# A decoder layer whose front runs in two passes of four token blocks instead of three of two, four and two

## The chip, the core and the metric

One core of a Trainium2 chip runs the whole layer as one launch. The metric is the device time of one execution in microseconds, the median of three runs. The core has five engines that run beside each other, each with its own list of instructions in a fixed order: PE (matmul), DVE (vector), ACT (scalar functions), POOL (here it only issues gathers) and SP (here it only issues transfers).

## The reference

Sequence 1024, width 1024, all float32. In short:

```python
h = x
h = h + hybrid_mixer(rms_norm(h, norm_mix), w_in, conv_w, ..., w_out)   # conv group + gated DeltaNet
h = h + memory_cross_attention(rms_norm(h, norm_x), rms_norm(mem, norm_mem), w_xq, w_xkv, w_xo)
h = h + peer_ffn(rms_norm(h, norm_ffn), w_query, sub_keys, expert_u, expert_v)
return rms_norm(h, norm_final)

def peer_ffn(xn, ...):            # 8 heads x 16 best of 128 x 128 experts: 128 rows for each token
    q = xn @ w_query; scores = q against two sets of 128 keys; two top-16, then top-16 of their sums
    u = expert_u[idx]; act = gelu(xn . u); y = sum(gate * act * expert_v[idx])
```

The DeltaNet part is a recurrence over the sequence: the state after one block of tokens goes into the next. `expert_u` and `expert_v` hold 16384 rows of 4 KB each.

## The kernel before

The 1024 tokens are eight blocks of 128. Four of them (2 to 5) get their experts densely: all 16384 experts are multiplied (`dense`), and a table of gates, written to DRAM by `densify`, zeroes those not chosen. The other four (0, 1, 6, 7) get their experts by gathering: for each token 128 rows of `expert_u` and 128 of `expert_v`, 512 KB for each slot of a block.

The front (everything up to the queries of the retrieval) runs per `Chunk` of blocks: `inproj` (28 weights of 128 columns from `w_in`), `invert` and `recur` (the recurrence, a pair of blocks at a time), `outproj`, `cross`, `queries`. Every weight of 512 KB is loaded by SP into `wraw`, split into `whi` by ACT (L242) and `wlo` by DVE (L244), and multiplied three times (L248 to L250). The chunks are blocks 0 and 1, then 2 to 5, then 6 and 7, so the front's weights pass three times, with 256, 512 and 256 columns.

`queries` ends with `best_keys`, where `top16` (L817 to L821) finds the best keys on DVE. `route_close` turns them into gates and row numbers. `gather_u` multiplies gathered rows with the token on DVE (L935). The sum over `expert_v` has two forms: `gather_v` adds row by row on DVE (L1020), `gather_p` lets PE multiply 32 columns of weights with the gathered rows, four products at once (L971), for two gathers. The bit mask `VD` says which blocks take DVE: 194 are blocks 1, 6 and 7. Gathered rows land in the pool `gp`, in `NG` = 6 buffers of 4 KB a partition. `densify` makes one-hot tiles on DVE (L1050 to L1053, in a tile of the pool `qp`, named `unit`) and multiplies them on PE (L1059).

The order on each engine: the parts are Python generators; `merge` takes steps of several of them in proportion to the numbers beside them, and `G1` to `G5` say how many of the 1036 gather steps go beside which part. `tc.high_priority` (in `at`) shifts the priority by which the framework's scheduler then places instructions. The engines obey the order that comes out of it; nothing overtakes.

Of the kernel before, what the change touches and what calls it, by code (L numbers as in the profile page):

```python
# [41 lines left out]
NSLIP, CLOSE, PACE = 4, 3, 517  # L42
G1, G2, G3, G4, G5 = 98, 90, 107, 17, 60
A5 = -1
C4, T5 = 61, 92
NSHORT, NRAW, NHI, NLO, NG, LU, LV, VD = 6, 3, 2, 2, 6, 1, 1, 194
PG1, PG2, PG3, PT, PR, PD = 100, -25, 0, 0, 0, 0
# [29 lines left out]
def merge(*gens):  # L77

    done = [0] * len(gens)
    live = [True] * len(gens)  # L80
    while any(live):
        j = min((i for i in range(len(gens)) if live[i]), key=lambda i: done[i] / gens[i][1])
        try:
            yield next(gens[j][0])
            done[j] += 1
        except StopIteration:
            live[j] = False


def run(*gens):  # L90
    for g in gens:
        for _ in g:
            pass
# [19 lines left out]
def _body(ctx, tc, I, out, dbg, front_only):  # L113
# [20 lines left out]
    def unit():  # L134
        return qp.tile([P, 4, T], F32, name="unit")
# [640 lines left out]

    def queries(c):

        t0, NB, T = c.t0, c.nb, c.T
        hv = c.h  # L780
        rstd = normalise(hv)
# [12 lines left out]
        for b in range(NB):  # L794
            routes[c.b0 + b] = Route(c.b0 + b)
        for hh in range(4):
            pair = []
            keys = sp.tile([P, 2, P], F32, name="keys")
            nc.sync.dma_start(keys, I["keysT"][:, 2 * hh:2 * hh + 2])
            for i in (2 * hh, 2 * hh + 1):  # L800
                ps = yield from proj_ct(I["w_pq"][i], x, T)
                pair.append(short()[:, :T])
                act(pair[-1], ps, AF.Copy)
                yield
            for b in range(0, NB, 2):
                yield from best_keys(c.b0 + b, hh, pair, keys, b * P)

# [217 lines left out]
    def densify(r, n):  # L1025
# [18 lines left out]
        for q in range(4):  # L1044
            st = [unit().rearrange("p a t -> p (a t)").rearrange("p (j t) -> p j t", t=32) for _ in range(2)]
            for v in range(0, 32, 8):
                ts = slice(32 * q + v, 32 * q + v + 8)
                hot = unit().bitcast(F16)
                oi, oj, *part = (hot[:, i].rearrange("p (g i t) -> p g i t", g=4, t=2) for i in range(4))
                tt(oi, iota8, pairs(num[:, 0, ts]), op=OP.is_equal)  # L1050
# [107 lines left out]

    ca, cb, cc = Chunk(0, 2), Chunk(2, 4), Chunk(6, 2)

# [5 lines left out]

    def tables(first):
        for n in range(4):
            yield from route_close(routes[first + n])
        for n in range(4):  # L1170
            yield from densify(routes[first + n], n)

# [10 lines left out]
    next(mem)  # L1183
    run(merge((invert(ca, (0, 1)), 17), (steps(mem, 13), 13)))
    run(merge((chain(recur(ca, 0), recur(ca, 1)), 10), (mem, 27)))
    run(chain(outproj(ca), cross(ca)))
    ib = inproj(cb)
    qa = queries(ca)
    if A5 >= 0:
        next(qa)  # L1190
        next(ib)
        run(merge((qa, 24), (steps(ib, A5), A5)))
    else:
        run(qa)
    if front_only:
# [3 lines left out]
    ga = at(pg, gathers(0))  # L1199
    tables2 = at("PT", tables(2))  # L1200
    for part, n, g in ((ib, 83 - max(A5, 0), G1), (recurrence(cb), 52, G2),
                       (chain(outproj(cb), cross(cb)), 59, G3)):
        run(merge((steps(ga, g), g), (part, n)))
    pg['now'] = 'PG2'
    banks["both"] = False
    qb = queries(cb)
    next(qb)
    rest = at("PR", chain(inproj(cc), recurrence(cc), outproj(cc), cross(cc), queries(cc)))
    run(merge((steps(ga, G4), G4), (qb, 32), (steps(rest, C4), C4)))
    run(merge((steps(ga, G5), G5), (tables2, T5), (rest, 195 - C4)))  # L1210

# [54 lines left out]
```

## Time and profile before

| | |
|---|---|
| median of three runs | 3339.02 us (3330.76 to 3339.60) |
| the profiled execution | 3335.89 us, span 3334.1 us |
| busy share of the span | PE 84%, DVE 81%, ACT 40%, POOL 40% |
| gathers (L918 and L964) | 1024, 536.94 MB of 890.34 MB in all |

The trace times start at the first instruction, and a stage is named by the weights that DVE begins to split at its start. The stages run from 0 to 370.6 (blocks 0 and 1), to 645.0 (input projection of blocks 2 to 5), to 886.4 (their recurrence), to 1064.0 (their output projection and attention), to 1348.0 (their queries mixed with the input projection of blocks 6 and 7), to 1577.0 and 1796.4 (the rest of blocks 6 and 7, beside the tables), to 3212.0 (dense part) and to the end.

### The profile page before, as it was taken

The page shows a single profiled execution, that of the slowest core. Times are in us where ns is not written, and L with a number is a line of the kernel's source. Part 1 is how long each engine was busy: PE and PEld are TensorE (multiplying, and loading weights), DVE is VectorE, ACT ScalarE, POOL GpSimd, SP SyncE. Part 2 cuts the span into 40 slices and gives each one's busy share as a digit, 9 for nine tenths or more (in the row PEclk, how much of TensorE's full clock was granted, in tenths as well). Part 3 has the DMA queues.
Part 4 walks back from the last instruction along what each step waited for, and adds up shares of the span by engine and source line. Part 5 has one row for each costly group of instructions (what it writes and reads, how often), then busy time and mean ns, then how long its engine had stood idle before and what let it go on. Part 6 is the DMA issues. An engine that isn't in the chain of part 4 may idle for free.

```text
span 3334.1 us, 42650 instructions
## 1 busy us (share of the span) xinstructions
PE 2784.7 (84%) x14826; PEld 2307.0 (69%) x14826; DVE 2693.7 (81%) x5527; ACT 1339.8 (40%) x2367; POOL 1324.6 (40%) x1028
## 2 busy tenths in 40 slices
PE   7898588877888877466777999999999999999950
PEld 7887466666555656465656888888888888888840
DVE  6654899978655788997668999888888888887888
ACT  5444333322232323334443554444444444444430
POOL 0000046746545441000000456556655555665665
PEclk9999788989998888788788999999999999999975
DMA  4344368959988884113455889999999999999998
GB/s 166 113 147 140 120 233 302 354 184 324 328 309 306 308 291 155 64 77 143 154 190 188 297 307 363 347 344 346 345 336 342 348 348 349 343 339 339 348 329 315
DMA packets 325495, 890.34 MB, mean 267 GB/s; under 512 B 27424, under 2 KB 96672, under 8 KB 321184
## 3 DMA queue, kind: packets, MB, share of 16 engines
q0 software_dynamic: 147456, 536.94, 44.3%
q1 hardware_dynamic: 177824, 350.69, 30.0%
q8 instruction: 116, 1.90, 0.2%
q14 instruction: 99, 0.81, 0.1%
HBM read 838.77 MB, written 48.76 MB: 266 GB/s over the span
## 4 chain that ended last, share of the span: by engine, by line
PE 43%; DVE 3%; issue 2%; DMA 1%; ACT 1%; POOL 1%; SPq 0%; POOLq 0%; DVEq 0%; ACTq 0%
PE ps L248 7%; PE ps L249 7%; PE ps L250 7%; PE po L248 7%; PE po L250 7%; PE po L249 7%; DMA g<-expert_v,g_ii 1%; POOL g L918 1%; DVE unit L1053 0%; DMA d_s<-kmd 0%; PE ps L1059 0%; DVE g_y L1020 0%; DVE wlo L244 0%; ACT whi L242 0%; DVE unit L1050 0%
## 5 line engine op out<-in xcount | busy, mean ns | idle before, releaser
L918 POOL DMA_INDIRECT g<-expert_u,g_ii x512 | 666.4, 1302 | 898.9 <-DVE t_s L820 434.4
L918 POOL DMA_INDIRECT g<-expert_v,g_ii x384 | 518.5, 1350 | 930.8 <-ACT g L1001 536.0
L242 ACT ACTIVATE whi<-wraw 128x1024 fp32r<-128x1024 f32 x452 | 479.9, 1062 | 836.0 <-PE ps L249 413.5
L244 DVE TENSOR_TENSOR wlo<-wraw,whi 128x1024 fp32r<-128x1024 f32 x452 | 552.4, 1222 | 321.7 <-ACT whi L242 319.4
L935 DVE SCALAR_TENSOR_TENSOR g<-g,xn 128x1024 f32<-128x1024 f32 x512 | 617.4, 1219 | 121.0 <-DMA g<-expert_u,g_ii 111.7
L250 PE MATMUL ps<-unit,wlo 128*128 128x512 f32 (+1 forms) x1784 | 653.3, 367 | 39.4 <-DVE wlo L244 39.3
L248 PE MATMUL ps<-unit,whi 128*128 128x512 f32 (+1 forms) x1784 | 659.1, 370 | 13.7 <-ACT whi L242 5.5
L249 PE MATMUL ps<-unit,whi 128*128 128x512 f32 (+1 forms) x1784 | 651.6, 365 | 0.0
L1020 DVE SCALAR_TENSOR_TENSOR g_y<-g,g_a,g_y 128x1024 f32<-128x1024 f32 x381 | 488.1, 1281 | 20.1 <-DMA g<-expert_v,g_ii 12.7
L249 PE MATMUL po<-wlo,unit 128*128 128x512 f32 x1136 | 444.0, 391 | 0.0
L250 PE MATMUL po<-whi,unit 128*128 128x512 f32 x1136 | 443.9, 391 | 0.0
L250 PEld LDWEIGHTS ps<-unit,wlo 128*128 128x128 f32 x1784 | 350.3, 197 | 98.6 <-DVE wlo L244 45.0
L248 PEld LDWEIGHTS ps<-unit,whi 128*128 128x128 f32 x1784 | 351.6, 197 | 76.7 <-ACT whi L242 11.0
L249 PEld LDWEIGHTS ps<-unit,whi 128*128 128x128 f32 x1784 | 351.5, 197 | 50.0 <-issue 0.8
L248 PE MATMUL po<-whi,unit 128*128 128x512 f32 x1136 | 383.1, 391 | 0.0
L249 PEld LDWEIGHTS po<-wlo,unit 128*128 128x128 f32 x1136 | 214.1, 188 | 48.3 <-issue 2.7
L250 PEld LDWEIGHTS po<-whi,unit 128*128 128x128 f32 x1136 | 214.0, 188 | 46.8 <-issue 2.5
L248 PEld LDWEIGHTS po<-whi,unit 128*128 128x128 f32 x1136 | 214.0, 188 | 45.8 <-issue 1.1
L1113 ACT ACTIVATE unit<-po 128x512 f32<-128x512 f32 x256 | 152.6, 597 | 150.1 <-PE po L250 144.8
L964 POOL DMA_INDIRECT g<-expert_v,g_y x128 | 139.4, 1089 | 161.3 <-DVE g L935 57.5
L1100 ACT ACTIVATE po<-unit 128x512 f32<-128x512 f32 x248 | 144.5, 605 | 0.0
L1059 PE MATMUL ps<-unit 128*128 128x128 f16 x1024 | 86.8, 239 | 52.3 <-DVE unit L1053 38.7
(391 smaller groups left out, 4053.1 us busy)
## 6 DMA issues: line engine op xcount, KB each, us to landing
wraw<-u_t SPq DMA_DIRECT2D x128, 512.0 KB, 7.1
wraw<-expert_v SPq DMA_DIRECT2D x128, 512.0 KB, 7.0
wraw<-w_in SPq DMA_DIRECT2D x84, 512.0 KB, 4.6
gd<-unit SPq DMA_DIRECT2D x32, 1024.0 KB, 5.9
unit<-gd SPq DMA_DIRECT2D x32, 1024.0 KB, 15.1
wraw<-w_out SPq DMA_DIRECT2D x24, 512.0 KB, 4.2
wraw<-w_xq SPq DMA_DIRECT2D x24, 512.0 KB, 4.4
wraw<-w_xo SPq DMA_DIRECT2D x24, 512.0 KB, 4.9
```

What stands on the lines that cost most here:

```text
L242: act(hi, raw, AF.Copy)
L244: tt(lo, raw, hi.bitcast(F32), op=OP.subtract)
L248: nc.tensor.matmul(ps, lh, rh, start=first, stop=False, skip_group_check=open_)
L249: nc.tensor.matmul(ps, lh, rl, start=False, stop=False, skip_group_check=open_)
L250: nc.tensor.matmul(ps, ll, rh, start=False, stop=last, skip_group_check=open_)
L918: nc.gpsimd.indirect_dma_start(out=g, out_offset=None, in_=I[table], in_offset=bass.IndirectOffsetOnAxis(ap=ii[:, k:k + 1], axis=0))
L935: stt(g, g, 1.0, xn, op0=OP.mult, op1=OP.mult, accum_out=r.a[:, k:k + 1])
L964: nc.gpsimd.indirect_dma_start(out=g, out_offset=None, in_=I["expert_v"], in_offset=bass.IndirectOffsetOnAxis(ap=iT[:, t:t + 1], axis=0))
L1020: stt(y, g, a[:, k:k + 1], y, op0=OP.mult, op1=OP.add)
L1059: nc.tensor.matmul(ps[:, u * P:(u + 1) * P], part[i][:, g, :, t], oj[:, g, :, t], start=i == 0, stop=i == 1)
L1100: act(pss[b], y[b][:, half * 512:(half + 1) * 512], AF.Copy)
L1113: act(y[b][:, half * 512:(half + 1) * 512], pss[b], AF.Copy)
```

## The change

The chunks become blocks 0 to 3 and 4 to 7. `queries` gets a first block and a count, since the second chunk does its retrieval in two halves: blocks 4 and 5, which go to the dense part, then 6 and 7. The tables of blocks 2 and 3 are made beside the recurrence of the second chunk, those of blocks 4 and 5 beside its last queries. The gathers of blocks 0 and 1 begin after the first chunk's queries, and 460 of their steps stand ahead of the dense part instead of 372. `VD` is 192, so block 1 is summed on PE like block 0. In `densify` the one-hot tile moves from the pool `qp` to two of the six buffers of the gathers.

```diff
-G1, G2, G3, G4, G5 = 98, 90, 107, 17, 60
-A5 = -1
-C4, T5 = 61, 92
-NSHORT, NRAW, NHI, NLO, NG, LU, LV, VD = 6, 3, 2, 2, 6, 1, 1, 194
+G1, G2, G3, G4, G5 = 100, 110, 140, 40, 70
+NSHORT, NRAW, NHI, NLO, NG, LU, LV, VD = 6, 3, 2, 2, 6, 1, 1, 192
...
-    def queries(c):
+    def queries(c, b0, NB):
...
-                hot = unit().bitcast(F16)
-                oi, oj, *part = (hot[:, i].rearrange("p (g i t) -> p g i t", g=4, t=2) for i in range(4))
+                hot = [gp.tile([P, D], F32, name="g").bitcast(F16) for _ in range(2)]
+                oi, oj, *part = (h[:, D * i:D * i + D].rearrange("p (g i t) -> p g i t", g=4, t=2)
+                                 for h in hot for i in range(2))
...
-    ca, cb, cc = Chunk(0, 2), Chunk(2, 4), Chunk(6, 2)
+    ca, cb = Chunk(0, 4), Chunk(4, 4)
...
-    def tables(first):
-        for n in range(4):
+    def tables(first, n0):
+        for n in range(2):
             yield from route_close(routes[first + n])
-        for n in range(4):
-            yield from densify(routes[first + n], n)
+        for n in range(2):
+            yield from densify(routes[first + n], n0 + n)
...
-    run(merge((invert(ca, (0, 1)), 17), (steps(mem, 13), 13)))
-    run(merge((chain(recur(ca, 0), recur(ca, 1)), 10), (mem, 27)))
+    run(merge((recurrence(ca), 52), (mem, 40)))
     run(chain(outproj(ca), cross(ca)))
...
+    run(queries(ca, 0, 4))
...
-    for part, n, g in ((ib, 83 - max(A5, 0), G1), (recurrence(cb), 52, G2),
-                       (chain(outproj(cb), cross(cb)), 59, G3)):
-        run(merge((steps(ga, g), g), (part, n)))
+    run(merge((steps(ga, G1), G1), (inproj(cb), 83)))
+    run(merge((steps(ga, G2), G2), (recurrence(cb), 52), (at("PT", tables(2, 0)), 38)))
+    run(merge((steps(ga, G3), G3), (chain(outproj(cb), cross(cb)), 59)))
+    banks["both"] = False
+    run(merge((steps(ga, G4), G4), (queries(cb, 0, 2), 17)))
     pg['now'] = 'PG2'
-    banks["both"] = False
-    qb = queries(cb)
-    next(qb)
-    rest = at("PR", chain(inproj(cc), recurrence(cc), outproj(cc), cross(cc), queries(cc)))
-    run(merge((steps(ga, G4), G4), (qb, 32), (steps(rest, C4), C4)))
-    run(merge((steps(ga, G5), G5), (tables2, T5), (rest, 195 - C4)))
+    run(merge((steps(ga, G5), G5), (at("PT", tables(4, 2)), 38), (queries(cb, 2, 2), 24)))
```

The new program's lines are two lower than the old ones from `queries` to `densify` and the matmuls and splits of the weights too (L242 is now DVE's split, L246 to L248 the three products, L933 and L1018 the gather sums, L969 the products of gathered rows), and one lower in `densify` (L1049 to L1052).

On DVE, in the recurrence of the chunk of four, the order before holds the steps of the chain alone at this place (L653 and L664 are the state's update, L638 a level of the inversion, L674 and L229 to L235 the norm):

```order
L653 SCALAR_TENSOR_TENSOR unit<-ps,ff,unit 128x128 x4
L638 TENSOR_TENSOR unit<-unit,po 128x512
L664 SCALAR_TENSOR_TENSOR state_104<-state_103,eg,ps 128x128 x4
L653 SCALAR_TENSOR_TENSOR unit<-po,ff,unit 128x128 x3
L674 TENSOR_TENSOR so<-so,fq_4813 128x4
L653 SCALAR_TENSOR_TENSOR unit<-po,ff,unit 128x128
L229 TENSOR_SCALAR rs_x<-so 128x4
```

The same place of the new program, where L1049 to L1052 are the one-hot steps of a table, L933 a gather sum and L955 the weights of the products on PE:

```order
L933 SCALAR_TENSOR_TENSOR g,g_a<-g,xn 128x1024
L662 SCALAR_TENSOR_TENSOR state_103<-state_104,eg,ps 128x128 x4
L933 SCALAR_TENSOR_TENSOR g,g_a<-g,xn 128x1024
L672 TENSOR_TENSOR so<-so,fq_5988 128x4
L1049 TENSOR_TENSOR g<-iota_84,z_n 128x1024
L1050 TENSOR_TENSOR g<-iota_84,z_n 128x1024
L955 TENSOR_TENSOR g_y<-g_y,masks 128x256
L227 TENSOR_SCALAR rs_x<-so 128x4
L1052 TENSOR_TENSOR g<-g,z_g 128x1024 x2
```

Table steps, written to buffers named `g`, and gather sums now stand between the steps of the chain.

On DVE at the end of the dense part, before, from the last two splits of weights (L244) on; the rows after these hold the finish of the dense blocks mixed with 70 more gather sums (L1020), the last of them 38 in a row:

```order
L244 TENSOR_TENSOR wlo<-wraw,whi 128x1024
L1020 SCALAR_TENSOR_TENSOR g_y<-g,g_a,g_y 128x1024 x4
L244 TENSOR_TENSOR wlo<-wraw,whi 128x1024
L1020 SCALAR_TENSOR_TENSOR g_y<-g,g_a,g_y 128x1024 x3
L1134 TENSOR_TENSOR unit<-unit 128x1024
L1020 SCALAR_TENSOR_TENSOR g_y<-g,g_a,g_y 128x1024
```

And in the new program (L242 the split, L1018 the gather sum, L997 the finish of block 7, L1133 that of the dense blocks):

```order
L242 TENSOR_TENSOR wlo<-wraw,whi 128x1024
L1018 SCALAR_TENSOR_TENSOR g_y<-g,g_a,g_y 128x1024 x3
L242 TENSOR_TENSOR wlo<-wraw,whi 128x1024
L1018 SCALAR_TENSOR_TENSOR g_y<-g,g_a,g_y 128x1024 x3
L997 TENSOR_TENSOR g_y<-g_y,g 128x1024
L1133 TENSOR_TENSOR unit<-unit 128x1024 x2
```

Behind the last split three gather sums are left, and none after the finish of the blocks.

On PE near the beginning of the dense part the new program has, between the products of the dense weights, groups of four products of gathered rows for block 1, which were not on PE before:

```order
L246 MATMUL ps<-unit,whi 128x512
L247 MATMUL ps<-unit,whi 128x512
L248 MATMUL ps<-unit,wlo 128x512
L969 MATMUL ps<-g,g_y 32x512 x4
L246 MATMUL po<-whi,unit 128x512
L247 MATMUL po<-wlo,unit 128x512
```

Such a group stands there 27 times; before, the dense part had none.

## Rows read from the trace of the kernel before

**Rows 1.** Busy time of each engine by stage.

```profile
core 0: us, PE busy (x) PEld busy (x) DVE busy (x) ACT busy (x) POOL busy (x), PEclk, DMA share, GB/s
0.00:370.60 370.60, 324.46 (x2262) 303.66 (x2263) 227.39 (x559) 173.32 (x346) 0.20 (x4) 0.94 0.44 151
370.60:645.00 274.40, 205.82 (x888) 166.87 (x888) 272.06 (x749) 87.98 (x130) 141.70 (x105) 0.84 0.70 249
645.00:886.40 241.40, 187.01 (x1249) 150.77 (x1248) 185.85 (x384) 59.98 (x159) 128.85 (x114) 0.89 0.78 279
886.40:1064.00 177.60, 152.54 (x690) 100.66 (x692) 102.18 (x209) 51.61 (x97) 86.62 (x80) 0.92 0.84 299
1064.00:1348.00 284.00, 219.24 (x1312) 172.82 (x1304) 233.03 (x905) 91.89 (x155) 99.97 (x89) 0.83 0.70 255
1348.00:1577.00 229.00, 134.43 (x1046) 118.90 (x1047) 206.38 (x563) 87.19 (x231) 0.00 (x0) 0.77 0.23 89
1577.00:1796.40 219.40, 160.90 (x1225) 135.37 (x1225) 155.78 (x397) 99.53 (x258) 0.00 (x0) 0.85 0.49 179
1796.40:3212.00 1415.60, 1400.26 (x6168) 1157.98 (x6166) 1206.08 (x1629) 683.31 (x985) 789.46 (x573) 0.99 0.94 336
3212.00:3334.10 122.10, 0.00 (x0) 0.00 (x0) 104.96 (x143) 4.99 (x10) 77.76 (x65) 0.51 0.87 315
```

**Rows 2.** POOL's timeline: start, us, what, and the idle time before it.

```profile
1822.15 0.94 POOL L918 DMA_INDIRECT g<-expert_v,g_ii  x1 [535.02 <-ACT g L1001]
```

**Rows 3.** Busy time in 100 us of the dense part, columns as in rows 1.

```profile
2400.00:2500.00 100.00, 100.00 (x443) 82.82 (x442) 81.01 (x110) 50.45 (x74) 59.85 (x43) 1.00 0.95 336
```

**Rows 4.** Gathers after 3212 us: ns min/median/max, first and last start.

```profile
L918 POOL DMA_INDIRECT g<-expert_v,g_ii x65: 933/1020/1922, 3212.0 to 3314.6; - x65
```

**Rows 5.** PE's timeline in the prefix.

```profile
59.88 0.28 PE L248 MATMUL po<-unit,whi 128*128 128x256 f32 x1
60.00 0.28 PE L249 MATMUL po<-unit,whi 128*128 128x256 f32 x1
```

**Rows 6.** PE groups by line, 104 to 370 us: busy us, mean ns, idle before.

```profile
L635 PE MATMUL ps<-unit 128*128 128x128 f32 x56 | 7.4, 275 | 0.0
...
L293 PE MATMUL po<-call,unit 128*128 128x128 f32 x16 | 6.8, 426 | 13.1 <-DVE unit L788 6.9 <-DVE unit L705 6.2
...
L632 PE MATMUL ps<-unit 128*128 128x128 f32 x32 | 4.3, 278 | 0.0
```

**Rows 7.** DVE groups by line over the whole span, columns as in rows 6.

```profile
L1053 DVE TENSOR_TENSOR unit<-unit,z_g 128x1024 f16<-128x1024 f16 x128 | 81.1, 683 | 0.0
...
L821 DVE FIND_INDEX8 p_topi<-p_top,t_s 128x8 uint16<-128x128 f32 x128 | 35.4, 283 | 0.0
...
L893 DVE TENSOR_REDUCE ki<-t_s 128x64 bf16<-128x1024 bf16 x16 | 19.4, 1214 | 0.2
```

**Rows 8.** PE's timeline at the start of the dense part.

```profile
1814.19 0.80 PE L248 MATMUL ps<-unit,whi 128*128 128x512 f32 x1
```

**Rows 9.** PE's timeline around one group of products of gathered rows.

```profile
860.23 1.07 PE L971 MATMUL po<-g,g_y 128*32 128x512 f32 x8
```

**Rows 10.** Line L971 on PE: what its idle time waited for (us, times).

```profile
  DMA g<-expert_v,g_y: 123.2, 43
```

**Rows 11.** Line L1136, the squares of the dense blocks.

```profile
L1136 ACT ACTIVATE unit<-unit x4: 1048/1057/1057, 3211.2 to 3221.9; 128x1024 f32<-128x1024 f32 x4
```

**Rows 12.** Timeline of POOL and DVE early in the dense part.

```profile
1841.23 1.21 DVE L244 TENSOR_TENSOR wlo<-wraw,whi 128x1024 fp32r<-128x1024 f32 x1
1841.31 1.95 POOL L918 DMA_INDIRECT g<-expert_v,g_ii  x1 [1.85 <-DVE rs_t L234]
...
1844.84 1.20 DVE L893 TENSOR_REDUCE ki<-t_s 128x64 bf16<-128x1024 bf16 x1
1845.11 0.94 POOL L918 DMA_INDIRECT g<-expert_v,g_ii  x1 [1.85 <-DVE rs_y L235]
```

**Rows 13.** Line L918 between 370 and 1300 us: issue to landing.

```profile
DMA to landing us min/median/max: 4.0/6.5/12.2
```

More of the change, by code (lines that the diff above doesn't have):

```diff
@@ L774, in cross @@
             dbgout("h2", hv[b], slice(c.t0 + b * P, c.t0 + (b + 1) * P))
-    def queries(c):
-        t0, NB, T = c.t0, c.nb, c.T
-        hv = c.h
+    def queries(c, b0, NB):
+        t0, T = c.t0 + b0 * P, NB * P
+        hv = c.h[b0:b0 + NB]
         rstd = normalise(hv)
@@ L794, in queries @@
         for b in range(NB):
-            routes[c.b0 + b] = Route(c.b0 + b)
+            routes[c.b0 + b0 + b] = Route(c.b0 + b0 + b)
         for hh in range(4):
@@ L805, in queries @@
             for b in range(0, NB, 2):
-                yield from best_keys(c.b0 + b, hh, pair, keys, b * P)
+                yield from best_keys(c.b0 + b0 + b, hh, pair, keys, b * P)
     class Route:
@@ L1183, in _body @@
     next(mem)
-    run(merge((invert(ca, (0, 1)), 17), (steps(mem, 13), 13)))
-    run(merge((chain(recur(ca, 0), recur(ca, 1)), 10), (mem, 27)))
+    run(merge((recurrence(ca), 52), (mem, 40)))
     run(chain(outproj(ca), cross(ca)))
[L1187 to L1194, printed above, removed]
+    run(queries(ca, 0, 4))
     if front_only:
@@ L1199, in _body @@
     ga = at(pg, gathers(0))
-    tables2 = at("PT", tables(2))
-    for part, n, g in ((ib, 83 - max(A5, 0), G1), (recurrence(cb), 52, G2),
-                       (chain(outproj(cb), cross(cb)), 59, G3)):
-        run(merge((steps(ga, g), g), (part, n)))
-    pg['now'] = 'PG2'
-    banks["both"] = False
-    qb = queries(cb)
-    next(qb)
-    rest = at("PR", chain(inproj(cc), recurrence(cc), outproj(cc), cross(cc), queries(cc)))
-    run(merge((steps(ga, G4), G4), (qb, 32), (steps(rest, C4), C4)))
-    run(merge((steps(ga, G5), G5), (tables2, T5), (rest, 195 - C4)))
+    run(merge((steps(ga, G1), G1), (inproj(cb), 83)))
[3 more added lines that the diff above has]
+    run(merge((steps(ga, G4), G4), (queries(cb, 0, 2), 17)))
+    pg['now'] = 'PG2'
+    run(merge((steps(ga, G5), G5), (at("PT", tables(4, 2)), 38), (queries(cb, 2, 2), 24)))
     pg['now'] = 'PG3'
```

## The prediction

> **What bounds the kernel now.** I read the busy time by stage first [rows 1], because the share over the whole span hides that the stages have different limits. Five stretches matter. Up to 370.6 us PE is busy 324.5 of 370.6 us and no expert row is gathered: this is the front of blocks 0 and 1 with the memory keys, and PE bounds it. From 370.6 to 1348 the front of blocks 2 to 5 runs beside the gathers of blocks 0 and 1; in its first stage DVE is busy 272.1 of 274.4 us, so DVE is the bound there. From 1348 to 1796 the front of blocks 6 and 7 runs beside the tables of blocks 2 to 5, and POOL does nothing at all: its timeline shows a gather that follows 535 us of idleness [rows 2]. From 1796 to 3212 the dense part runs, with PE busy 1400.3 of 1415.6 us: 443 matmuls in 100 us at full clock, 0.2257 us each [rows 3]. The last stretch, 122.1 us, has no matmul. There the rest of the gathers runs out, 65 of them [rows 4]. So the end is set by PE through the dense part, and then by gathers that were late, while 450 us ahead of it passed without one.
>
> **The change part by part.** The sum is made against the profiled execution, 3335.9 us with a span of 3334.1; the median is 3339.0, so I add 3 us at the end. What stands where in the new program is counted in its order; all durations are from rows.
>
> *Prefix, four blocks instead of two.* The 28 input weights now meet 512 columns instead of 256. A 256-column matmul starts 0.12 us after the one before [rows 5], one of 512 columns takes 0.2257 us [rows 3]: 672 x 0.106 = 71 us. Queries of attention and retrieval: 384 x 0.106 = 41. Both output projections: 192 more at 0.2257 = 43. A second pair of blocks through inversion and recurrence: the lines of its three level products are busy 36 us in this stretch for one pair, in six rows of which the first and the last stand in [rows 6]; with the other lines about 55. Transposes, scores, values and keys of two more blocks: about 40 (eight rows, L293 the largest, [rows 6]). Sum 250. If PE's idle 46 us stay as they are, the prefix ends at 621; if they grow in step, at 656 (250 x 370.6/324.5 = 286). Wider products hide more of the weight splitting, so I lean to the first: **630**, range 605 to 656. All of this is cost: there are no gathers beside it.
>
> *Input projection of blocks 4 to 7, 100 gathers.* DVE-bound at 99% before [rows 1]. The order puts 86 more top-16 instructions there (17 searches of five instructions up to 0.28 us each [rows 7], 1.4 us) and a few more gather products: 274 + 24 = **298** (288 to 310).
>
> *Recurrence beside the tables of blocks 2 and 3.* Before, 241.4 us with DVE busy 185.9. One table is 16 steps of four DVE instructions of 0.684 us [rows 7], 44 us; one closing of a route has six reduces of 1.21 us [rows 7], ten products of 0.68, and eight searches, about 25. The stage gets two tables and somewhat over one closing, 114 us. If they all fall into DVE's idle 55.5 us, 300; if none does, 355. Gathers stay at some 143. I take **330**.
>
> *Cross attention.* 109 gathers instead of 81. The stage moved 299 GB/s for 177.6 us [rows 1], 53 MB; 28 more of 0.52 MB make 68 MB, and at the 336 GB/s of the dense part [rows 1] 202 us. With all hidden, 178. I take **193**.
>
> *Queries of blocks 4 to 7, tables of 4 and 5.* The order holds here 352 top-16 instructions (about 90 us), 120 table steps (82), 68 instructions of closings (40), 27 gather sums (33), 16 splits (20) and smaller ones (20): 285 us added up, some 245 of busy time since neighbours overlap, and 126 gathers; with weights, table writes and row copies about 96 MB, 286 us at 336 GB/s. I take **285** (250 to 310). This replaces the mixed stage and the whole third pass: there 284 + 229 + 219 = 732 us went [rows 1], now 285 plus what the other stages were charged. The third pass's 52 weight splits go with it.
>
> So the dense part begins at 630 + 298 + 330 + 193 + 285 = 1736, 60 us earlier.
>
> *Dense part.* Its 6144 matmuls are unchanged. Before, the first came at 1814.2 [rows 8], 18 us after the stage's start; 81 fewer small DVE instructions stand there now, so 10. From there PE worked 1397 us, until just short of 3212. New inside: 27 groups of products for block 1, whose row sum was on DVE. One group takes 1.07 us [rows 9], its last 0.07 beside the next matmul; 27 us in all. PE takes instructions in order, so it may wait for gathers: before, 43 waits on these rows cost 123.2 us over 64 groups [rows 10], so 27 groups cost up to 52. But PE was then early and is now late, and in the order a group stands only every 24 matmuls (5.4 us). I take 5: dense 1397 + 32 = **1429**. DVE is relieved of 128 x 1.28 us, worth nothing by itself since PE is the bound.
>
> *Tail.* Before, 74 gather sums stand behind the last weight split on DVE; now three do. So the 122.1 us shrink to what the dense part itself needs at its end: four squares over 11 us [rows 11], the scaling and the last write, about 21; with the last summed block **27** (21 to 45). What was late is done earlier: 460 gather steps ahead of the dense part instead of 372. The density beside the dense part is unchanged, 18 or 19 sums for eight weights.
>
> Sum: 1736 + 10 + 1429 + 27 = 3202 of span against 3334.1, or 132 us less: front 60, head of the dense part 8, tail 95, less 32 on PE. 3339 - 132 = **3207**.
>
> *A rule that speaks against it.* Tables now run beside gathers. In the trace a gather issued under the two-input weight split takes 1.95 us, one under a reduce with one input 0.94 us [rows 12]. The Trainium skill says in "SBUF — State Buffer", section Who interferes with whom, that a DVE instruction with two SBUF inputs contends with a GpSimd instruction that reads SBUF. The trace agrees as far as it shows issues; no row shows one under a table step, whose four instructions all have two inputs. Without it the sum stays; by it, case 4 below.
>
> **The rivals.**
> 1. *The tables and the gathers block each other.* The one-hot tiles of a table used to lie in the unit pool; now they take two of the six buffers of the gathers. In the new program 43 of 128 such tiles take a buffer whose last reader is a product of gathered rows on PE. DVE then waits for PE, PE for a landing (median 6.5 us, [rows 13]), and behind the table step on DVE stand weight splits and recurrence. 43 waits at the 2.9 us of [rows 10] are 125 us, at a whole landing 280; in the middle, 4.7 us, 202: 3207 + 202 = **3409**, slower. It decides from 3.1 us each (132 / 43). Against it: the order puts other work between. Chance 0.12.
> 2. *DVE fills its gaps.* The tables have no DMA ahead of them, so DVE runs at 99% as in the input projection: prefix 621, stages 298, 300, 185, 255: 1659 instead of 1736, **3130**. For it: 272.1 of 274.4 us there. Against: recurrence is a chain between PE, ACT and DVE. Chance 0.17.
> 3. *The products of block 1 hold up the dense part.* With the full 52 us of waits and the tail at its upper bound, 47 + 18 more: **3272**. For: DMA is at 0.94 there. Chance 0.12.
> 4. *Issue becomes the limit of the last front stage.* If beside tables each issue takes 2.0 us, as the 1.95 us under the weight split, and 0.3 between, 126 gathers need 290 us, and with the thirteen gathers of lead 320: 35 more, **3242**. This is the case by the rule above. Chance 0.04.
>
> **How the numbers follow.** My forecast has 0.55. The lowest bounds of all terms together give 3080, the highest 3370; as they will not all fall to one side, I take 3115 to 3330, which holds the forecast with its bounds and cases 2 to 4, and leaves out case 1 and the ends. A measurement of this kernel can tell about 0.3%, 10 us, from no change. Slower: case 1 beyond 3.3 us each, 0.12. Within 0.3%: its milder form, 0.06. Faster: 0.82.
>
> **What would show it.** Right: a busy table whose prefix ends near 630, a recurrence stage with DVE above 90%, a first dense matmul near 1745, dense stages at 443 matmuls per 100 us after the first 130 us, and under 45 us behind the last matmul. Wrong: DVE waiting on PE at the table's first product (L1049 of the new program), PE waiting on gathered rows inside the dense part, or a prefix beyond 660.

## The result and the profile after

| | before | after |
|---|---|---|
| median of four runs | 3339.31 us (3330.76 to 3339.85) | 3367.85 us (3361.95 to 3379.98) |
| profiled execution, its span | 3335.89 us, 3334.1 us | 3362.69 us, 3360.9 us |

The change makes the kernel 1% slower: ratio 1.0096, 95% interval 1.0078 to 1.0114 (this ratio and those below are taken over all runs, not from the medians). The forecast was 3207 us, in a range that ended at 3330. In the text `after` is the new program. Its busy table has one row for each term of the sum (span; busy us of PE, PE's weight loads, DVE, ACT, POOL, each with its count; granted clock; DMA share; GB/s): prefix, input projection of blocks 4 to 7, recurrence beside tables, cross attention, last front stage, head of the dense part (from DVE's first split of a dense weight to the first dense matmul), dense matmuls, tail.

```profile
core 0: us, PE busy (x) PEld busy (x) DVE busy (x) ACT busy (x) POOL busy (x), PEclk, DMA share, GB/s
0.00:656.50 656.50, 580.75 (x3140) 496.04 (x3140) 345.57 (x889) 240.15 (x456) 0.20 (x4) 0.94 0.27 92
656.50:955.60 299.10, 216.07 (x915) 172.71 (x916) 297.11 (x913) 93.11 (x146) 144.80 (x110) 0.82 0.68 238
955.60:1323.40 367.80, 240.60 (x1740) 194.06 (x1739) 294.55 (x630) 102.48 (x286) 130.41 (x117) 0.80 0.66 232
1323.40:1525.40 202.00, 167.88 (x758) 105.61 (x758) 118.72 (x234) 52.02 (x97) 118.12 (x106) 0.88 0.91 328
1525.40:1863.60 338.20, 194.71 (x1374) 117.39 (x1373) 256.92 (x902) 88.43 (x206) 133.86 (x118) 0.72 0.78 281
1863.60:1895.90 32.30, 23.45 (x161) 12.55 (x158) 20.52 (x79) 11.42 (x25) 12.34 (x12) 0.81 0.95 353
1895.90:3337.00 1441.10, 1433.80 (x6360) 1155.28 (x6360) 1121.93 (x1469) 676.73 (x973) 769.41 (x562) 1.00 0.91 326
3337.00:3361.00 24.00, 0.00 (x0) 0.00 (x0) 17.65 (x72) 6.01 (x11) 0.00 (x0) 0.57 0.27 110
```

Beside the forecast:

| term | forecast | measured | difference |
|---|---|---|---|
| prefix | 630 | 656.5 | +26 |
| input projection | 298 | 299.1 | +1 |
| recurrence and tables | 330 | 367.8 | +38 |
| cross attention | 193 | 202.0 | +9 |
| last front stage | 285 | 338.2 | +53 |
| head of the dense part | 10 | 32.3 | +22 |
| dense matmuls | 1429 | 1441.1 | +12 |
| tail | 27 | 24.0 | -3 |
| span | 3202 | 3361 | +159 |

Against the kernel before, [rows 1]: the prefix grew by 286 us (370.6 to 656.5). The rest of the front shrank by 204 (from 370.6 to the first dense matmul at 1814.19, [rows 8], 1443.6; now 1239.4). The dense part grew by 44, the tail shrank by 99. That is +27 of span. So the tail's gain came in full, the dense part took back almost half of it, and the front with the head of the dense part, which was to win 68 us, lost 82.

How the last front stage runs is best seen in a stretch of its chain of work (start, length, what; pieces under 1 us left out), and in who waited there (engine, line and tile, for whom: total us, times, longest).

```profile
1618.93 5.20 DMA g<-expert_v,g_y
1624.27 1.99 PE ps L969 x8
1626.46 7.91 DMA g<-expert_v,g_y
1634.41 2.01 PE ps L969 x8
1639.32 5.79 DMA g<-expert_v,g_y
1645.15 2.01 PE ps L969 x8
```

```profile
PE ps L969 <- DMA g<-expert_v,g_y: 88.0, 25, 9.7
POOL g L962 <- PE ps L969: 55.2, 23, 7.0
POOL g L962 <- PE ps L1058: 47.0, 15, 10.5
...
DVE g L1049 <- PE ps L969: 26.3, 9, 6.8
```

A gather lands, PE multiplies its rows (a group of four products, which the trace shows as eight records, x8), which frees two buffers, POOL issues the next gathers into them, and PE waits for these in turn. POOL waits for a buffer that PE still holds, for a product of rows (L969) or of a table (L1058); DVE waits for one with its first one-hot tile (L1049); and everything that stands behind the waiting product on PE waits as well. No engine bounds the stage: DVE is busy 256.92 of 338.2 us, PE 194.71, DMA has a share of 0.78.

### The profile page after: what moved, and what is told of

The parts are those of the page before. It is cut to its first block, busy times and chain, and to the rows that moved or that the text cites. A ratio compares the mean times of both kernels' runs of the same rounds, so it can differ in the third digit from the quotient of the medians.

```text
span 3360.9 us, 41036 instructions
## 1 busy us (share of the span) xinstructions
PE 2857.2 (85%) x14440; PEld 2253.6 (67%) x14440; DVE 2473.0 (74%) x5178; ACT 1270.3 (38%) x2198; POOL 1309.2 (39%) x1028
## 4 chain that ended last, share of the span: by engine, by line
PE 47%; DMA 7%; DVE 5%; issue 2%; POOL 1%; ACT 0%; SPq 0%; ACTq 0%; POOLq 0%; DVEq 0%
PE ps L246 7%; PE ps L248 7%; PE ps L247 7%; PE po L246 7%; PE po L248 7%; PE po L247 7%; DMA g<-expert_v,g_y 4%; PE ps L969 2%; DMA g<-expert_u,g_ii 1%; DVE g L933 1%; POOL g L962 1%; DVE g L1052 1%; DMA wraw<-expert_v 0%; DVE wlo L242 0%; DMA unit<-g_ffn_row 0%
## 5 line engine op out<-in xcount | busy, mean ns | idle before, releaser
L242 DVE TENSOR_TENSOR wlo<-wraw,whi 128x1024 fp32r<-128x1024 f32 x400 | 489.7, 1225 | 429.8 <-ACT whi L240 421.2
L933 DVE SCALAR_TENSOR_TENSOR g<-g,xn 128x1024 f32<-128x1024 f32 x512 | 618.9, 1219 | 138.7 <-DMA g<-expert_u,g_ii 119.5
L248 PE MATMUL ps<-unit,wlo 128*128 128x512 f32 (+1 forms) x1512 | 584.5, 387 | 25.6 <-DVE wlo L242 25.5
L246 PE MATMUL ps<-unit,whi 128*128 128x512 f32 (+1 forms) x1512 | 587.4, 389 | 4.6 <-ACT whi L240 4.5
L247 PE MATMUL ps<-unit,whi 128*128 128x512 f32 (+1 forms) x1512 | 583.4, 386 | 0.0
L962 POOL DMA_INDIRECT g<-expert_v,g_y x256 | 290.3, 1134 | 446.1 <-PE ps L969 162.9
L916 POOL DMA_INDIRECT g<-expert_v,g_ii x256 | 361.7, 1413 | 261.5 <-DVE g_y L1018 188.6
L248 PE MATMUL po<-whi,unit 128*128 128x512 f32 x1168 | 455.1, 390 | 0.0
L246 PE MATMUL po<-whi,unit 128*128 128x512 f32 x1168 | 403.6, 393 | 3.1 <-ACT unit L335 1.7
L248 PEld LDWEIGHTS ps<-unit,wlo 128*128 128x128 f32 x1512 | 293.8, 194 | 90.4 <-DVE wlo L242 35.2
L246 PEld LDWEIGHTS ps<-unit,whi 128*128 128x128 f32 x1512 | 294.3, 195 | 78.8 <-ACT whi L240 13.3
L247 PEld LDWEIGHTS ps<-unit,whi 128*128 128x128 f32 x1512 | 293.6, 194 | 57.6 <-issue 2.5
L1018 DVE SCALAR_TENSOR_TENSOR g_y<-g,g_a,g_y 128x1024 f32<-128x1024 f32 x254 | 325.7, 1282 | 3.4 <-DMA g<-expert_v,g_ii 1.3
L246 PEld LDWEIGHTS po<-whi,unit 128*128 128x128 f32 x1168 | 219.6, 188 | 62.3 <-issue 8.3
L248 PEld LDWEIGHTS po<-whi,unit 128*128 128x128 f32 x1168 | 219.5, 188 | 46.5 <-issue 0.8
L969 PE MATMUL ps<-g,g_y 128*32 128x512 f32 x768 | 132.9, 747 | 111.3 <-DMA g<-expert_v,g_y 104.4
L1058 PEld LDWEIGHTS <-g 128*128 128x128 f16 x1024 | 74.4, 109 | 141.2 <-DVE g L1052 108.3
```

The costliest lines, as they stand in the source:

```text
L242: tt(lo, raw, hi.bitcast(F32), op=OP.subtract)
L246: nc.tensor.matmul(ps, lh, rh, start=first, stop=False, skip_group_check=open_)
L247: nc.tensor.matmul(ps, lh, rl, start=False, stop=False, skip_group_check=open_)
L248: nc.tensor.matmul(ps, ll, rh, start=False, stop=last, skip_group_check=open_)
L916: nc.gpsimd.indirect_dma_start(out=g, out_offset=None, in_=I[table], in_offset=bass.IndirectOffsetOnAxis(ap=ii[:, k:k + 1], axis=0))
L933: stt(g, g, 1.0, xn, op0=OP.mult, op1=OP.mult, accum_out=r.a[:, k:k + 1])
```

## The experiments

Each changes `after`, unless said otherwise, and all compute the whole layer. The letters of the theories are those of the expectations. The one that stands at the end, for the last front stage above all, is D: where gathers run beside other work, the number of row buffers under way sets their pace, since a buffer is taken from the issue until its last reader is through.

**hot_own**: do tables and gathers block each other because they share six buffers (case 1)? The one-hot tiles get two buffers of their own, and four stay for the gathers.

```diff
-NSHORT, NRAW, NHI, NLO, NG, LU, LV, VD = 6, 3, 2, 2, 6, 1, 1, 192
+NSHORT, NRAW, NHI, NLO, NG, LU, LV, VD = 6, 3, 2, 2, 4, 1, 1, 192
...
-hot = [gp.tile([P, D], F32, name="g").bitcast(F16) for _ in range(2)]
+hot = [gp.tile([P, D], F32, name="hot", bufs=2).bitcast(F16) for _ in range(2)]
```

> The changed kernel with the one-hot tiles of the tables in two buffers of their own and the gathers in four buffers instead of six; nothing else differs. In the changed kernel the recurrence stage took 368 us and the last front stage 338 us, where the forecast had 330 and 285; DVE waited 53 us at the table's first product and POOL 59 us for the table products on PE to give back a buffer. Theory A (tables and gathers block each other through the shared six buffers): these waits go, the last front stage falls to 290 us or less and the recurrence to 345 or less; the first dense matmul comes 60 us earlier than 1896, near 1835. Theory B (PE, in order, waits for the gathered rows of blocks 0 and 1): PE's waits on gathered rows stay near 317 us or grow, since fewer gathers are under way; the first dense matmul stays within 25 us of 1896. With four buffers the dense part may be slower; that is read apart, by its stages of eight weights.

3554 us, 1.0636 (1.0594 to 1.0678). Recurrence and last front stage, columns as above, and PE's wait for rows in the last stage (88.0 us in 25 waits in `after`):

```profile
924.20:1369.60 445.40, 264.79 (x1782) 210.95 (x1781) 336.38 (x702) 105.30 (x293) 182.36 (x160) 0.77 0.71 242
1578.10:2008.60 430.50, 213.43 (x1394) 126.25 (x1398) 268.47 (x929) 90.32 (x207) 143.32 (x134) 0.64 0.70 243
```

```profile
PE ps L969 <- DMA g<-expert_v,g_y: 167.3, 35, 11.5
```

Taking the sharing away while the sum stays at six makes it 186 us worse. A's gain does not come; PE's waits for rows grow, as B said, but the first dense matmul comes some 150 us after 1896, not within the 25 that B allowed. The run changes two things at once, the sharing and the number of buffers for rows (six to four), so it does not show what sharing alone costs; too few buffers for the rows may be the harm. (The direct undoing, the one-hot tile back in its old pool, was not tried, so what that move alone costs stays open.)

**block1_dve**: block 1 summed on DVE again.

```diff
-NSHORT, NRAW, NHI, NLO, NG, LU, LV, VD = 6, 3, 2, 2, 6, 1, 1, 192
+NSHORT, NRAW, NHI, NLO, NG, LU, LV, VD = 6, 3, 2, 2, 6, 1, 1, 194
```

> The changed kernel with block 1 summed on DVE, as before the change. Theory B: PE's waits on gathered rows fall from 317 us in 94 waits to about 123 us, what block 0 alone cost before; the last front stage gets 70 more DVE sums (90 us) but loses PE's waits of 91 us, so it stays at 310 to 340; the dense part loses its 27 groups, so from its first to its last matmul about 1400 us instead of 1441; time about 3325. Theory A: the one-hot tiles still share the buffers, with gathers that DVE reads; DVE no longer waits for PE at the table's first product, but the gathers still wait for table products; time about 3340. If neither is right (the front is simply longer than was counted) the first dense matmul comes later than 1896, by the 90 us of DVE sums.

3364 us, 1.0079 (1.0055 to 1.0102), the same as `after`. The last front stage is 29 us longer and the dense part 31 us shorter:

```profile
1526.40:1893.30 366.90, 159.74 (x1130) 118.17 (x1128) 325.63 (x941) 90.82 (x211) 158.44 (x121) 0.64 0.75 265
1928.70:3338.30 1409.60, 1400.81 (x6146) 1154.96 (x6144) 1186.01 (x1552) 675.91 (x974) 767.03 (x559) 1.00 0.93 332
```

Neither theory's time came. PE's own waits for rows fall from 148.1 us in 46 waits to 92.7 in 28 over the whole kernel, but DVE's work in the last stage grows by 69 us: a wait of one engine is exchanged for work of another.

**before_block1_pe**: that part alone, in the kernel before.

```diff
-NSHORT, NRAW, NHI, NLO, NG, LU, LV, VD = 6, 3, 2, 2, 6, 1, 1, 194
+NSHORT, NRAW, NHI, NLO, NG, LU, LV, VD = 6, 3, 2, 2, 6, 1, 1, 192
```

> The kernel before with block 1 summed on PE and nothing else of the change. There block 1's gathers run beside the dense part alone, so 64 groups of products stand among the dense matmuls. By the forecast's price (1.07 us a group, and nearly no wait, as PE comes late) 68 us more on PE and a tail that stays at 122 us: 3405. Theory B (PE waits for each group, 2 to 3 us, also in the dense part): 130 to 190 us more on PE: 3470 to 3530. Theory A has no part in it and expects what the forecast's price gives.

3424.5 us, 1.0266 (1.0246 to 1.0286). All 64 groups of products fall into the dense part:

```profile
1818.20:3305.30 1487.10, 1479.66 (x6658) 1157.47 (x6658) 1048.03 (x1429) 678.35 (x978) 786.36 (x579) 1.00 0.90 321
```

That is 90 us more than 1397, 1.4 us for a group, with PE idle for only 7 of 1487 us: the products cost mostly by their work, not by waits. At the 1.20 us by which a group moves the next matmul back (measured below) 64 groups are 77 us; the other 13 were not placed. The time lies between the forecast's price (3405) and theory B's (3470 and more), nearer the first. So this part alone makes the kernel before slower; in `after` 27 of the groups are left in the dense part.

**no_gather_last**: the 70 steps of gathers beside the last front stage are left to the dense part.

```diff
-G1, G2, G3, G4, G5 = 100, 110, 140, 40, 70
+G1, G2, G3, G4, G5 = 100, 110, 140, 40, 0
...
-run(merge((steps(ga, G5), G5), (at("PT", tables(4, 2)), 38), (queries(cb, 2, 2), 24)))
+run(merge((at("PT", tables(4, 2)), 38), (queries(cb, 2, 2), 24)))
```

> The changed kernel with the 70 gather steps taken away from the last front stage and left to the dense part and its tail. Theories A and B both expect that stage to fall from 338 us to what DVE and PE need without gathers, 250 to 275 us; the tail then takes the 70 steps at 1.9 us, 130 us more. If the stage stays above 300 us, neither the buffers nor the gathered rows are the cause, but the stage's own work was counted too small.

3400.7 us in one run. Two views: the busy row of the stage, and L1049 on DVE (busy us, mean ns, idle before it and what ended that), first of `after`, then of this kernel:

```profile
1518.80:1785.40 266.60, 160.03 (x1146) 124.06 (x1145) 248.73 (x865) 87.65 (x207) 57.78 (x52) 0.67 0.60 223
```

```profile
L1049 DVE TENSOR_TENSOR g<-iota,z_n 128x1024 f16<-128x1024 f16 x30 | 20.6, 686 | 42.4 <-PE ps L969 26.3 <-PE ps L1058 16.2
```

```profile
L1049 DVE TENSOR_TENSOR g<-iota,z_n 128x1024 f16<-128x1024 f16 x32 | 21.6, 676 | 0.1
```

DVE's work is nearly unchanged (248.73 against 256.92), but the stage is 72 us shorter: 66 gathers fewer, 1.1 us each. PE's work falls by 35 us and POOL's by 76, but neither engine is the bound; DVE's idle time falls by 63 us. DVE's waits at the tables' first step are gone. The dense part (1495.7) and the tail (99.5) are 130 us longer in return: late, the same gathers, with their products, cost 2.0 us each. It was right to do them early; they only aren't free there.

**product_later**: the product of a row pair issued one step after its gather, so that PE meets it when it has landed.

```diff
+def late(W=W, u=u, gs=gs, q=q):
...
     with tc.issue_after(product(1, 0).ins):
         product(1, 1)
         product(0, 0)
         product(0, 1)
+if pend:
+    pend.pop()()
+pend.append(late)
```

> The changed kernel with the four products of a pair of gathered rows issued one pair later, after the next pair's gathers; nothing else. Theory C (PE in order: it stands before a product until its rows land, and the queries' and tables' matmuls stand behind it): the rows have a whole pair's time more to land, PE's waits on gathered rows fall from 317 us to under 150, the last front stage from 338 to 310 or less, the first dense matmul from 1896 to about 1865, time about 3335. Theory D (the six buffers bound how many gathers are under way): two more buffers are held while waiting for the later product, so POOL waits longer for a buffer; PE's waits do not fall by half and the last front stage stays at 338 or grows.

3365.2 us, 1.0090 (1.0065 to 1.0115): the same as `after`. The last front stage takes 346.4 us, and PE waits there 107.7 us for rows in 26 waits, against 88.0 in 25. POOL waits 120 us instead of 102 for the buffers of PE's products. So C falls, and D's expectation came: a later product holds its two buffers longer, and the next gather starts later.

**seven_buffers**, with **four_short** as its control: a seventh buffer, for which the pool of short tiles is cut from six to four (first diff); and the cut alone (second).

```diff
-NSHORT, NRAW, NHI, NLO, NG, LU, LV, VD = 6, 3, 2, 2, 6, 1, 1, 192
+NSHORT, NRAW, NHI, NLO, NG, LU, LV, VD = 4, 3, 2, 2, 7, 1, 1, 192
```

```diff
-NSHORT, NRAW, NHI, NLO, NG, LU, LV, VD = 6, 3, 2, 2, 6, 1, 1, 192
+NSHORT, NRAW, NHI, NLO, NG, LU, LV, VD = 4, 3, 2, 2, 6, 1, 1, 192
```

> The changed kernel with seven buffers of 4 KB for gathers and one-hot tiles instead of six; their room comes from two of the six short tiles of the front, so the front may lose a little by that alone. Theory D: one more gather under way; with four buffers beside two for the tables the recurrence took 445 us and the last front stage 430, with six shared 368 and 338, so with seven some 340 and 310, the first dense matmul near 1840. Theory C: PE stands before the same products; all stages within 15 us of the changed kernel.

> After with the pool of short tiles cut from six to four and the six gather buffers kept: the control for seven_buffers, which did both. Theory D: no gain, 3365 to 3375, so the 13 us of seven_buffers belong to its seventh buffer (and more, if the short pool costs something). Rival F: the smaller pool itself, by holding DVE's steps back, gives the gain: 3350 to 3358.

**five_buffers**: one buffer fewer, the pool of short tiles as in `after`.

```diff
-NSHORT, NRAW, NHI, NLO, NG, LU, LV, VD = 6, 3, 2, 2, 6, 1, 1, 192
+NSHORT, NRAW, NHI, NLO, NG, LU, LV, VD = 6, 3, 2, 2, 5, 1, 1, 192
```

> After with five gather buffers instead of six (two of them are taken by each table step as before). Theory D (the buffers under way set the rate of the gathers wherever gathers and tables share a stage, and the in-order engines DVE and PE stand waiting for rows there): the seventh buffer gave 13 us, hot_own's four cost 186, so the fifth lies between: 3400 to 3470, with the recurrence stage at 385 to 420 us and the last front stage at 360 to 400. Rival F (buffers are not the limit; hot_own was slow for another reason, for instance where its tiles lie): 3360 to 3380, stages as in after.

| buffers | median us | ratio to before | recurrence and tables | last front stage |
|---|---|---|---|---|
| 5 (five_buffers) | 3491.4 | 1.0471 (1.0451 to 1.0491) | 417.6 | 397.6 |
| 6 (after) | 3367.9 | 1.0096 (1.0078 to 1.0114) | 367.8 | 338.2 |
| 6 (four_short) | 3370.1 | 1.0105 (1.0084 to 1.0127) | 357.7 | 345.8 |
| 7 (seven_buffers) | 3355.0 | 1.0056 (1.0035 to 1.0076) | 345.8 | 305.2 |

The rows of these two stages, and PE's wait for rows in the last one, of five_buffers and then of seven_buffers:

```profile
938.20:1355.80 417.60, 254.14 (x1740) 205.62 (x1739) 313.29 (x658) 104.31 (x287) 143.48 (x131) 0.76 0.64 221
1585.90:1983.50 397.60, 210.62 (x1365) 122.42 (x1363) 261.09 (x908) 90.23 (x207) 136.65 (x123) 0.63 0.71 248
...
PE ps L969 <- DMA g<-expert_v,g_y: 151.5, 34, 9.9
```

```profile
973.50:1319.30 345.80, 238.94 (x1770) 195.33 (x1769) 275.89 (x599) 105.64 (x298) 120.86 (x110) 0.85 0.66 233
1523.90:1829.10 305.20, 194.38 (x1349) 124.23 (x1347) 252.99 (x904) 88.98 (x206) 121.38 (x108) 0.72 0.82 297
...
PE ps L969 <- DMA g<-expert_v,g_y: 62.2, 19, 8.5
```

The last stage goes 398, 338 to 346, 305 with the count of buffers, while DVE's work stays at 253 to 261 us. A sum makes it plain. In `after` 118 gathers and 30 table steps of two tiles pass there, 178 tiles through six buffers in 338.2 us: each takes up a buffer for 11.4 us, the time that it stands empty before the next tile included. In five_buffers 183 tiles take 10.9 us each, in seven_buffers 168 take 12.7; in hot_own 134 gathers alone pass four buffers at 12.9. From five to seven there are 40% more buffers, and this time grows by 17%: the count sets most of the pace. The traces also allow a direct reading, gathers and readers paired by their order: from the start of a gather's issue (or of a table step's first instruction) to the end of the last sum or product that reads the buffer, the mean is 9.6 us with five buffers, 9.9 with six, 10.8 with seven, and the buffers are so taken for 86 to 88% of the stage in all three.

D stands for the last stage, F falls, and the control shows that the pool of short tiles did nothing for the time as a whole. D's numbers did not all come: both stages of five_buffers lie in the range given for them, its time 21 us above; seven_buffers begins the dense part at 1861.5, not near 1840. In the recurrence the count matters less: the same sum gives 10.7, 12.2 and 13.9 us there, and part of what the stage gains is that fewer gathers fall into it (131, 117, 110). Of the 33 us that the last stage gains from the seventh buffer some 11 are those of ten gathers that now stand further ahead (the input projection takes 319.1 us); the dense part begins 34 us earlier in all. Most of that is lost again, since the dense part takes 1472.1 us instead of 1441.1; the reason was not isolated (before_seven shows the same).

**no_gather_recur**: no gather beside recurrence and tables.

```diff
-G1, G2, G3, G4, G5 = 100, 110, 140, 40, 70
+G1, G2, G3, G4, G5 = 100, 0, 140, 40, 70
...
-run(merge((steps(ga, G2), G2), (recurrence(cb), 52), (at("PT", tables(2, 0)), 38)))
+run(merge((recurrence(cb), 52), (at("PT", tables(2, 0)), 38)))
```

> The changed kernel with no gather step beside the recurrence of the second chunk; the 110 steps there are left out of the front and come later. The gather sums of that stage (71, or 82 us of DVE) go with them, so DVE's work is about 215 us. If gathers cause the stage's length: 368 falls to 240 to 260. If the chain of the recurrence and the tables on PE cause it: it stays above 300.

3471.6 us in one run. The stage:

```profile
947.70:1208.10 260.40, 201.28 (x1603) 184.55 (x1602) 229.75 (x514) 103.84 (x297) 31.92 (x27) 0.88 0.36 135
```

107 us less for 90 gathers less (27 are left), at the upper end of what was expected if gathers cause the length. DVE's work falls by 65 us, of which 50 sums of `gather_u` (L933, 72 against 22) are 61; the other 42 are waits. Again the gathers cost more later: the last front stage is 25 us longer, the dense part and its tail together 200.

**tables_by_cross**: the tables of blocks 2 and 3 beside output projection and cross attention instead of the recurrence.

```diff
-run(merge((steps(ga, G2), G2), (recurrence(cb), 52), (at("PT", tables(2, 0)), 38)))
-run(merge((steps(ga, G3), G3), (chain(outproj(cb), cross(cb)), 59)))
+run(merge((steps(ga, G2), G2), (recurrence(cb), 52)))
+run(merge((steps(ga, G3), G3), (chain(outproj(cb), cross(cb)), 59), (at("PT", tables(2, 0)), 38)))
```

> The changed kernel with the tables of blocks 2 and 3 beside the cross attention of the second chunk instead of beside its recurrence. In the changed kernel the recurrence has DVE busy 294.6 of 367.8 us and waits 40 us for gathered rows, and cross attention has DVE busy 118.7 of 202.0. If DVE's idle time there can be filled: recurrence 241 to 260 as before the change, cross attention 235 to 260, together 490 to 510 instead of 570, time 3290 to 3310. If idle time on DVE is not to be had because DVE, in order, waits for gathered rows in both stages: the 114 us of tables only change places, together 550 to 580, time 3350 to 3380.

3347.6 us, 1.0023 (1.0001 to 1.0045), 20 us better than `after`. The recurrence, then cross attention:

```profile
948.80:1225.00 276.20, 196.38 (x1275) 150.91 (x1273) 227.03 (x520) 66.60 (x165) 149.89 (x125) 0.84 0.76 263
1225.00:1502.00 277.00, 208.61 (x1177) 138.40 (x1175) 179.52 (x336) 85.51 (x207) 114.10 (x100) 0.86 0.78 277
```

553 us for both, instead of 570: the second of the two expectations by the stages, 2 us below its range by the time. Wherever the tables stand beside gathers they lengthen the stage, here by 92 and 75 us; the recurrence is the worse place.

**cross_and_seven**: tables_by_cross and seven_buffers together.

> Tables of blocks 2 and 3 beside the output projection and cross attention as in tables_by_cross, and seven gather buffers as in seven_buffers. Theory D: two separate gains, 20 and 13 us, that add: 3328 to 3342, equal to the kernel before within 0.3 per cent. Rival G (both remove the same wait, DVE and PE standing for rows beside the tables of blocks 2 and 3): no more than the better of the two, 3345 to 3352.

3333.7 us, 0.9993 (0.9981 to 1.0004). The gains add, as D said and G did not; the kernel then takes as long as the kernel before.

**before_seven**: the seventh buffer in the kernel before, whose table steps take their tiles from another pool.

```diff
-NSHORT, NRAW, NHI, NLO, NG, LU, LV, VD = 6, 3, 2, 2, 6, 1, 1, 194
+NSHORT, NRAW, NHI, NLO, NG, LU, LV, VD = 4, 3, 2, 2, 7, 1, 1, 194
```

> The kernel before with seven gather buffers and four short tiles, nothing else. Theory D holds for it only where gathers lie beside other work: its table steps take their tiles from the unit pool, so all seven are free for gathers; the tail of 122 us and the waits for rows shrink: 3300 to 3325. Rival F: PE bounds its front and its dense part, the rows wait for DVE and not for a buffer: 3327 to 3345, as before.

3323.9 us, 0.9967 (0.9947 to 0.9988): 0.3% faster than the kernel before and the fastest of all, just inside D's range. The cut of the short tiles has no control in this kernel. Dense matmuls and tail, of before_seven and then of before:

```profile
1811.90:3242.60 1430.70, 1409.20 (x6144) 1153.10 (x6144) 1231.74 (x1570) 675.59 (x977) 855.63 (x607) 1.00 0.95 343
3242.60:3310.20 67.60, 0.00 (x0) 0.00 (x0) 60.85 (x109) 6.02 (x11) 35.07 (x29) 0.53 0.79 295
```

```profile
1814.20:3210.80 1396.60, 1395.12 (x6146) 1154.07 (x6144) 1187.08 (x1535) 678.38 (x977) 789.43 (x572) 1.00 0.95 339
3210.80:3334.10 123.30, 0.00 (x0) 0.00 (x0) 106.16 (x144) 6.18 (x11) 77.78 (x65) 0.51 0.87 315
```

The front is as long as before. 35 more gathers fit beside the dense part, and the tail shrinks by 56 us; the dense part itself grows by 34. This profile is of the fastest of twelve executions (3312.0 us), so it shows about twice the gain of the medians. The DMA share is 0.95 in both, and ACT waits 49.7 us for weights to arrive instead of 18.7, PE 20.8 us for splits instead of 1.3: rows that come earlier take their time from weights. That is how I read it, no run isolates it.

## Why the prediction was wrong, step by step

**Prefix: 26 us too short.** The work was right: PE is busy 580.75 us, and 324.46 [rows 1] plus the 250 of the sum is 574. The step that failed is that PE's idle time would stay at 46 us. It is 75.7, about in step with the work, and the bound I named for that was 656. What PE waits for there was not followed up. There is no gather beside it, so its 286 extra us were paid in full.

**Input projection, tail: right.** 299.1 and 24.0 us. DVE is the bound of the first with 297.11 us busy, as before, and the late gathers are gone from the second.

**Recurrence beside tables: 38 too short, and last front stage: 53 too short. This is the step that decided.** Both were added up from DVE's work and a DMA rate. The work was right: I had 300 (185.9 and 114) and 245 us busy, and it is 294.55 and 256.92. What failed is the step from work to time: 330 lay between tables wholly inside DVE's idle time (300) and not at all (355), and the stage took longer than either; 285 stood on the 336 GB/s of the dense part, and the stage moved 281 GB/s. What the sum had no term for is the buffer: a tile takes one up for some 11 us, two are taken by each table step, and six are all there are. With 66 of 118 gathers gone the last stage is 72 us shorter (no_gather_last), with 90 of 117 gone the recurrence 107 (no_gather_recur); 63 and 42 of these are idle time of DVE. five_buffers and seven_buffers show that the last stage's time hangs on the number of buffers. Seven buffers still leave both stages 16 to 20 us above the forecast. Moving the one-hot tile from another pool into these six put 62 table steps, 124 tiles, on top of 235 gathers in these two stages.

**Case 1 had the place, but only a part of the mechanism.** It named the shared buffers and gave 3409 us. DVE does wait there, but 52 us in 19 waits, where the case asked for 202 us in 43; beside it stand PE's wait for rows and POOL's for a buffer. And hot_own, which removes the sharing but leaves four buffers to the rows, is worse. Its reading of [rows 10], which the dense part and case 3 share, was also off: the 123.2 us in 43 waits count the weight load of the same product a second time. The product alone waits:

```profile
PE po L971 <- DMA g<-expert_v,g_y: 31.5, 13, 9.1
PE ps L971 <- DMA g<-expert_v,g_y: 25.2, 8, 6.3
```

that is 56.7 us in 21 waits before, and in `after` 148.1 in 46 (the 317 us in 94 waits of the expectations are these, counted twice):

```profile
PE ps L969 <- DMA g<-expert_v,g_y: 104.4, 31, 9.7
...
PE po L969 <- DMA g<-expert_v,g_y: 43.7, 15, 6.1
```

All but one of these, 2.9 us in the head of the dense part, lie in the front; among the dense matmuls, where case 3 looked for them, there is none.

**Case 2** (DVE fills its gaps) is refuted: DVE is busy 80% in the recurrence and 76% in the last stage. **Case 4**: POOL's gathers take 133.86 us for 118 in the last stage, 1.13 us each, where the case asked for 2.0; in the other 204 us POOL issues nothing, 102 of them in the two waits for PE's buffers shown above. The Trainium skill says in "SBUF — State Buffer", section Who interferes with whom, that a DVE instruction with two SBUF inputs contends with a GpSimd instruction that reads SBUF. The last stage of `after` agrees: a gather whose issue begins under the table steps L1049 and L1052 takes 1.33 and 1.21 us (medians of 12 and 13), one beside an idle DVE 0.94; but no limit comes of it here.

**Cross attention: 9 too short.** The upper bound, 202, came, with 106 gathers and 328 GB/s at a share of 0.91. That looks like a DMA bound, but seven_buffers passes 116 gathers there in about the same time, so the buffers have a part in it too:

```profile
1319.30:1523.90 204.60, 172.15 (x777) 105.32 (x777) 124.77 (x244) 52.29 (x97) 126.40 (x116) 0.87 0.95 352
```

**Head of the dense part: 22 too short.** I counted DVE's small instructions. PE is busy 23.45 of these 32.3 us with other work, six groups of products of gathered rows (48 records) and the last table and query products among it, which had not been done in the stage ahead.

**Dense part: 12 too short.** The size of one term was off: a group of products took 1.0 us in the sum. PE's timeline (start, length) around one, between dense matmuls:

```profile
1965.13 0.39 PE L248 MATMUL po<-whi,unit 128*128 128x512 f32 x1
1965.44 1.07 PE L969 MATMUL ps<-g,g_y 128*32 128x512 f32 x8
1966.44 0.50 PE L246 MATMUL po<-whi,unit 128*128 128x512 f32 x1
1966.78 0.39 PE L247 MATMUL po<-wlo,unit 128*128 128x512 f32 x1
```

From 1965.13 to 1966.78 lie two dense matmuls, 0.2257 us each [rows 3], and the group: 1.20 us. 27 of them are 32 us, where the sum had 27. The 5 us that I had set down for waits on rows did not come; PE waits 4.7 us at 2134 us for DVE's split of a weight instead. So of the 44 us that the dense part is longer than before, 32 are the groups and 5 this gap; some 7 us I could not place.

## What to carry over

Where gathered rows lie beside other work, write one more line into the sum: tiles that pass the pool, times the time that one is held (landing, use, and the wait of an engine that works in order), divided by the buffers; a stage can't be shorter than that, however idle its engines are. Take the holding time from a trace with about as many buffers, since it grew somewhat with their number here. Before other tiles move into such a pool, change its size by one in both directions, since that shows at once whether it is the limit. And a gain at the end of a kernel bought with a longer beginning has to pay for the time in which nothing runs beside it: here the tail gave 99 us and the prefix took 286, of which the shorter front gave back 204.

## What was not expected of the hardware

In the last front stage PE is busy 194.71 of 338.2 us and the granted clock is 0.72 in the mean. In the stretch of the chain above PE is busy 12.05 of 34 us, and the clock is 0.50:

```profile
1616.00:1650.00 34.00, 12.05 (x50) 2.89 (x50) 17.82 (x61) 2.06 (x5) 13.59 (x13) 0.50 0.82 282
```

That is the lower of its two levels, 1.2 and 2.4 GHz. A group of products takes 1.99 to 2.01 us there; in the dense part, with PE busy throughout and the clock at 1.00, it takes 1.07. So in this stretch PE, which waits for rows, also multiplies them more slowly, and holds their buffers 0.9 us longer. The mean granted clock of that stage is 0.72 with seven buffers, 0.72 with six and 0.63 with five; how much of the lost time is the clock's was not measured.
